# A hybrid attention and MLP layer on one core: fp32 scores ahead of the rounded ones, and transposes gathered into fewer breaks

## The chip, the core and the metric

The kernel runs on one of the cores of a Trainium2 chip. The core has a matrix engine, TensorE (PE), with a queue of weight loads that runs ahead of its matmuls (PEld), and VectorE (DVE), ScalarE (ACT), GpSimd (POOL) and SyncE (SP). TensorE writes only to PSUM, which is eight banks of 128 partitions by 512 fp32 columns. The metric is the device time of one execution in microseconds, as the median of several runs.

## The reference

256 rows of 1024 channels go through one decoder layer, all in fp32:

```python
h = rmsnorm(x, norm1_g)
proj = h @ w_in                      # q, k/v of 3 branches, gates, q/k/v of the second mixer, 2 merge gates
# mixer A: 8 heads; compressed keys (p_cmp), selected blocks, sliding window, gated and summed
y_nsa = gc[0] * (p_cmp @ vc) + gc[1] * (p_sel @ vs) + gc[2] * (p_win @ vw)
# mixer B: 8 heads of block attention; at 256 rows one block, so causal attention
y_moba = softmax(mask(qm @ km.T / 8)) @ vm
mixed = sig(g_A) * (y_nsa @ w_up_nsa) + sig(g_B) * (y_moba @ w_up_moba)
x = x + mixed @ w_out
u = relu(rmsnorm(x, norm2_g) @ w_ff1)
x = x + (u * u) @ w_ff2
return rmsnorm(x, norm_f_g)
```

## The kernel before

**Matmuls.** Large products are made in a rounded format (F32R) in three parts: each operand is split into a high part (rounded, by ScalarE, line 121) and a low part (the rest, by VectorE, line 123), and `mm3` issues high x high, high x low and low x high. Small products, the first 128 rows' scores and all transposes are plain fp32. A plain fp32 matmul appears in the trace as two instructions, a transpose as one.

**Chunks and slots.** The weights come in 60 chunks. Slot c is the run of matmuls that uses chunk c: `run_slot` walks over them (24 wide ones in the projections) and between them issues whatever was registered by `at(pos, f, ...)`, in order of `pos`: an event goes out before the first matmul whose share of the slot has reached its position. With 24 matmuls, all positions above 0.083 and up to 0.125 fall before the fourth matmul, and their order among each other is that of `pos`. Each engine works through its instructions in that program order and waits by semaphores. Such a place where PE leaves its matmuls for something else is called a break here.

**Splitting and loading.** In slot c, `std_events` and `split_events` register the high parts (`hs`) and low parts (`ls`) of the two halves of chunk c + 2, and, 0.05 behind the later low part, the load of chunk c + 5 on SP's queue: its buffer is that of chunk c + 2, so it waits for those low parts. A low part given a position above 1 is not registered there.

**Units.** Attention runs in six units d = 0 to 5, of two head pairs each. Unit d's scores are in slot 9 + 2d: `d_scores` writes tiles Sa and Sb (two banks each, one buffer each): the first 128 rows against 128 keys in fp32 (columns 0 to 127), the other rows against 256 keys rounded (columns 128 to 383). Each matmul has 64 rows of contraction, so that two use the halves of the array. Then `d_max` (VectorE: mask and maxima), `d_exp` (ScalarE), `d_norm` (VectorE, next slot); in the next odd slot `d_trans` transposes P into the same Sa and Sb, and copies them out, Sa by ScalarE (line 595), Sb by VectorE (line 596); only then can the next unit's scores be written. `d_pv` multiplies with the values a unit later. Slots 9 and 11 also transpose the second mixer's q and k (`transp_heads`, four transposes into each of two banks, line 386). The probabilities of the compressed branch, `pcs`, are transposed in slot 8 (`cmp_probs_t`, line 524) and used from slot 13 on.

**Mixed rows.** Slots 20 to 23 multiply with the two up-projections. `upn_evac` and `upm_evac` (VectorE, lines 801 to 808) merge them by the gates into `sgs[0]`, for t = 0 and 1 (the halves of the rows). `mix_t(t, i, ...)` transposes four 128-column blocks of rows t and columns half i (line 815) and makes the high part (`mxh`, ScalarE, line 819); `mix_l` makes the low part (`mxl`, VectorE, line 823). Slot 24, the first of w_out, begins with half 0 and takes half 1 in its second half.

Of the kernel before, what the change touches and what calls it, by code (L numbers as in the profile page):

```python
# [42 lines left out]
def hybrid_layer(ctx: ExitStack, tc: tile.TileContext, firstd, gxd, w, w1c, small, const, gf, out):  # L43
# [30 lines left out]
    def tp_tile():  # L74
        return next_bank("tp")
# [261 lines left out]
    def std_events(c):  # L337
        if c == 9:
            split_events(c, (0.0, 0.06), (0.09, 0.46))
        elif c == 11:  # L340
            split_events(c, (0.0, 0.1005), (0.1008, 0.1015))
        elif 9 < c < 22 and c % 2:
            split_events(c, (0.0, 0.1005), (0.09, 0.1015))
        elif 9 <= c < 20:
            split_events(c, (0.0, 0.45), (0.3, 0.8))
        else:
            split_events(c, (0.0, 0.45), (0.3, 0.46))
# [30 lines left out]
    def early_bank(t):  # L378
        return ps_e.tile([128, 512], F32, name=f"kvbacc{t}")

    def transp_heads(src, dst, i, q=True, early=None):

        tp = tp_tile() if early is None else early_bank(early)
        for j in range(2):
            for t in range(2):
                pe.transpose(tp[:, j * 256 + t * 128:j * 256 + t * 128 + 128],
                             src[:, t, (2 * i + j) * 128:(2 * i + j + 1) * 128], ident)
        v = tp.rearrange("p (a q) -> p a q", a=2)
        ps = slice(2 * i, 2 * i + 2)
        if not isinstance(dst, tuple):  # L390
            act.activation(dst[:, ps, :], v, AF.Copy)
            return
        split_evac(v, tuple(d[:, ps, :] for d in dst), q)
# [124 lines left out]
                          gates[:, 0].rearrange("q p t h -> q t p h"), op=ALU.mult)  # L518
        dve.tensor_tensor(s, s, row(3), op=ALU.mult)

    def cmp_probs_t():
        tp = tp_tile()
        for t in range(2):
            pe.transpose(tp[:, t * 128:(t + 1) * 128], pcs[:, t].rearrange("q p c -> q (p c)"),
                         ident)
        act.activation(pcT, tp[:, 0:256], AF.Copy)


    yTh = {m: ap_.tile([128, 4, 256], F32R, name=f"yTh{m}") for m in "nm"}
# [4 lines left out]

    def d_scores(d):
        S = [s_tile(x) for x in range(2)]
        rows = [slice(j * 64, (j + 1) * 64) for j in range(2)]
        late = []
        for x, (kind, p, b) in enumerate(PAIRS[d]):
            qs = qrT if kind == "n" else qmT  # L540
            kk, kp = (ksT if b == 1 else kwT, 0) if kind == "n" else (kmT, p)
            for i, (a, b_) in enumerate(((1, 1), (1, 2), (2, 1))):
                for j, r in enumerate(rows):
                    mm(S[x][:, j, 128:384], qs[a][r, p, :], kk[b_][r, kp, :], i == 0, i == 2)
            late += [(S[x][:, j, 0:128], qs[0][r, p, :], kk[0][r, kp, :])
                     for j, r in enumerate(rows)]
        for o, l, r in late:
            mm(o, l, r, True, True)
        U[d] = {"S": S, "P": ap_.tile([128, 4, 384], F32, name="P"),
                "st": ap_.tile([128, 4, 8], F32, name="ust", bufs=2)}  # L550

# [157 lines left out]
    for sec, c0, n in groups:  # L709
        if sec in ("q", "qm", "km"):  # L710
            tm[sec] = ap_.tile([128, 2, 512], F32, name="qtm", bufs=2)
        if sec == "q":
            accs = [ps_e.tile([128, 512], F32, name=f"{sec}acc{t}") for t in range(2)]
        else:
            accs = [acc_tile(), acc_tile()]
        for i in range(2):
            c = c0 + i
            if c == 4:
                for t in range(2):
                    at(0.0, evac_tm, "kvb", t, second[t], 408)  # L720
                at(0.02, cmp_gather, 0)
                at(0.02, cmp_gather, 1)
                at(0.1, split, 5, 0, 2, "l")
                at(0.2, rope, kva, 2)
                at(0.3, split, 5, 1, 2, "l")
                at(0.35, load, 8)
                at(0.72, cmp_mlp1)
                split_events(c, (0.73, 0.78), (0.8, 0.9))
            elif c == 7:
                split_events(c, (0.0, 0.1), (0.2, 0.21))  # L730
            elif c == 5:
                split_events(c, (0.115, 0.45), (0.3, 0.46))
            else:
                std_events(c)
            unit_events(c)
            v_events(c)
            if c == 5:
                at(0.05, gate_evac)
                at(0.1, transp_k, kva, ksT)
                at(0.11, cmp_gelu)  # L740
                at(0.12, rope, kvb[:, :, 0:128], 2)
                at(0.13, cmp_gelu_end)
                at(1.0, cmp_mlp2)
                at(1.0, transp_k, kvb[:, :, 0:128], kwT, 0)
            if c == 6:
                at(0.6, load_x, 0, 16 + 1024)
                at(0.68, transp_heads, tm["q"], qT, 0)
                at(0.68, transp_heads, tm["q"], qT, 1)
                at(0.7, rope, tm["q"], 8)
            if c == 7:  # L750
                at(0.25, cmp_scores)
                at(0.25, transp_heads, tm["q"], qrT, 0, True, 0)
                at(0.25, transp_heads, tm["q"], qrT, 1, True, 1)
                at(0.25, cmp_softmax)
            if c == 8:
                at(0.35, cmp_probs_t)
                at(0.3, rope, tm["qm"], 8)
            if c == 9:
                at(0.12, transp_heads, tm["qm"], qmT, 0)
                at(0.12, transp_heads, tm["qm"], qmT, 1)  # L760
            if c == 10:
                at(0.5, rope, tm["km"], 8)
            if c == 11:
                at(0.102, transp_heads, tm["km"], kmT, 0, False)
                at(0.102, transp_heads, tm["km"], kmT, 1, False)
            if i == 1:
                at(0.49, evac_tm, sec, 0, accs[0], n)
                at(1.0, evac_tm, sec, 1, accs[1], n)
            run_slot(xstat(c, n, accs, range(4 * i, 4 * i + 4)))
# [56 lines left out]
    for sec, c0, kind, evac in (("upn", C_UPN, "n", upn_evac), ("upm", C_UPM, "m", upm_evac)):  # L826
        for i in range(2):
            c = c0 + i
            if c == C_UPN:
                split_events(c, (0.3, 0.3), (0.4, 0.4))  # L830
            elif c < C_UPM:
                std_events(c)
            elif c < C_UPM + 1:
                split_events(c, (0.0, 0.0), (0.1, 0.1))
            else:
                split_events(c, (0.0, 0.0), (9, 9))
            unit_events(c)
            v_events(c)
            for f, a in prev:
                at(0.02, f, *a)  # L840
            accs = [acc_tile(), acc_tile()]
            mms = []
            for t in range(2):
                for k in range(4):
                    lh, ll = (a[kind][:, k, t * 128:(t + 1) * 128] for a in (yTh, yTl))
                    mms += mm3(accs[t], lh, ll, hi[c][:, k * 512:(k + 1) * 512],
                               lo[c][:, k * 512:(k + 1) * 512], k == 0, k == 3)
            if c == C_UPM:
                at(0.95, lambda: mix_t(0, 0, bank("yb", "yb")))
                at(0.95, mix_l, 0, 0)  # L850
            elif c > C_UPM:
                at(0.49, lambda: mix_t(1, 0, s_tile(0)[:, 0]))
                at(0.6, mix_l, 1, 0)
            at(0.52, evac, 0, i, accs[0])
            run_slot(mms)
            prev = [(evac, (1, i, accs[1]))]
# [71 lines left out]
    for i in range(4):  # L928
        c = C_WOUT + i
        if i == 0:  # L930
            at(0.03, lambda: mix_t(0, 1, bank("yb", "yb")))
            at(0.04, mix_l, 0, 1)
            at(0.25, lambda: mix_t(1, 1, s_tile(1)[:, 0]))
            at(0.26, mix_l, 1, 1)
            lo_late(0.35, c - 1)
        elif i == 1:
            lo_late(0.03, c - 1)
        split_events(c, (0.0, 0.1), ((9, 9), (0.3, 0.3), (0.3, 0.3), (9, 9))[i])
        for f, a in prev:
            at(0.02, f, *a)  # L940
        v_events(c)
        if i == 1:
            at(0.01, open_ff)
        if i == 3:
            outs = [acc_tile()[:, 0:256] for _ in range(2)]
            at(0.52, wout_evac, i, outs, (0,))
            run_slot([m for j in range(2)
                      for m in wstat(outs[j], c, j * 128, 8, 256, mxh, mxl)])
            prev = [(wout_evac, (i, outs, (1,)))]
        else:  # L950
            mms, outs, _ = two_blocks(c, mxh, mxl, 4 if i == 0 else 8, i == 0)
            run_slot(mms)
            prev = [(wout_evac, (i, outs))]
# [375 lines left out]
```

## Time and profile before

| | |
|---|---|
| Median of 3 runs | 368.4 us (367.5 to 368.4) |
| The profiled execution | 367.42 us |
| Its span, first to last instruction | 365.6 us |
| PE busy | 358.9 us (98%) |
| DVE / ACT busy | 291.7 us (80%) / 245.2 us (67%) |
| Mean granted TensorE clock | 0.995 |
| HBM read / written | 94.57 MB / 22.54 MB |

The span is what the profile sees; the device time has 1.8 us around it. Times in a timeline are from the span's start. A matmul's length in a timeline includes its way through the array, so neighbours overlap and the pace is read from their starts. The chain of work that ended last is followed back from the last instruction, at each step to what released it; its pieces follow each other without overlap, which makes their lengths good for sums.

### The profile page before, as it was taken

How to read it: one execution, taken by the hardware profiler on the slowest of the kernel's cores; microseconds unless marked ns; L12 is line 12 of the kernel's file. 1: busy time of each engine (PE TensorE's matmuls, PEld its weight loads, DVE VectorE, ACT ScalarE, POOL GpSimd, SP SyncE). 2: the span in 40 equal slices, each digit the busy share in tenths (PEclk: the TensorE clock that was granted, in tenths of full speed). 3: DMA queues.
4: the chain of work that ended last, by engine and by line, in shares of the span. 5: the costliest groups of instructions: out<-in, count | busy, mean ns of one | idle time of the engine just before them, and what ended most of it. 6: DMA issues, size and time to landing. Idle time of an engine off the chain costs nothing.

```text
span 365.6 us, 6186 instructions
## 1 busy us (share of the span) xinstructions
PE 358.9 (98%) x2370; PEld 317.6 (87%) x2370; DVE 291.7 (80%) x481; ACT 245.2 (67%) x415; POOL 49.5 (14%) x72
## 2 busy tenths in 40 slices
PE   8999999999999999999999999999999999999993
PEld 8987788888888888788999999999999888888883
DVE  5989778889786777857866788888883979999995
ACT  5976665766757557435366788888877787777814
POOL 2033003222412231313320000000000000000000
PEclk9999999999999999999999999999999999999998
DMA  8999998999999989998797765565745699999603
GB/s 259 393 396 339 321 343 256 305 261 292 266 316 249 339 169 330 231 298 192 206 350 271 233 230 162 186 229 176 261 170 174 199 326 359 367 357 341 236 0 116
DMA packets 23805, 96.01 MB, mean 263 GB/s; under 512 B 2592, under 2 KB 3616, under 8 KB 18272
## 3 DMA queue, kind: packets, MB, share of 16 engines
q1 hardware_dynamic: 14544, 73.69, 55.0%
q0 software_dynamic: 8800, 21.50, 26.9%
q10 hardware_dynamic: 432, 0.44, 0.3%
q8 instruction: 18, 0.29, 0.3%
q14 instruction: 11, 0.09, 0.1%
HBM read 94.57 MB, written 22.54 MB: 320 GB/s over the span
## 4 chain that ended last, share of the span: by engine, by line
PE 89%; DVE 4%; DMA 3%; ACT 2%; issue 1%; DVEq 0%; SPq 0%
PE acc L285 60%; PE P L285 7%; PE o L285 6%; PE qacc L285 3%; PE kvbacc L285 2%; PE yb L285 2%; DMA raw<-in_ff_dram 2%; PE Sa L285 2%; ACT whi L121 1%; PE Sb L594 1%; PE Sa L594 1%; PE Sb L285 1%; DVE x L1131 1%; PE tp L285 1%; DVE gx L1139 1%; DMA g0x<-in_first_dram 1%
## 5 line engine op out<-in xcount | busy, mean ns | idle before, releaser
L121 ACT ACTIVATE whi<-raw 128x1024 fp32r<-128x1024 f32 (+3 forms) x112 | 115.0, 1046 | 41.4 <-PE acc L285 20.9
L123 DVE TENSOR_TENSOR wlo<-raw,whi 128x1024 fp32r<-128x1024 f32 (+3 forms) x112 | 131.6, 1206 | 11.6 <-ACT whi L121 10.7
L285 PE MATMUL acc<-h2h,wlo 128*128 128x256 f32 x256 | 70.8, 276 | 0.0
L285 PE MATMUL acc<-h2l,whi 128*128 128x256 f32 x256 | 70.7, 276 | 0.0
L285 PE MATMUL acc<-h2h,whi 128*128 128x256 f32 x256 | 70.7, 276 | 0.0
L285 PE MATMUL acc<-whi,hTh 128*128 128x512 f32 (+1 forms) x128 | 49.5, 392 | 0.2 <-ACT whi L121 0.2
L285 PE MATMUL acc<-wlo,hTh 128*128 128x512 f32 (+1 forms) x128 | 48.6, 384 | 0.0
L285 PE MATMUL acc<-whi,hTl 128*128 128x512 f32 (+1 forms) x128 | 48.5, 384 | 0.0
L285 PEld LDWEIGHTS acc<-h2h,wlo 128*128 128x128 f32 x256 | 48.1, 188 | 0.0
L285 PEld LDWEIGHTS acc<-h2h,whi 128*128 128x128 f32 x256 | 48.1, 188 | 0.0
L285 PEld LDWEIGHTS acc<-h2l,whi 128*128 128x128 f32 x256 | 48.1, 188 | 0.0
L285 PEld LDWEIGHTS acc<-whi,hTh 128*128 128x128 f32 x128 | 23.9, 188 | 5.3 <-ACT whi L121 0.6
L1032 DVE TENSOR_TENSOR sql<-ur,sqh 128x512 fp32r<-128x512 f32 x16 | 11.1, 693 | 21.6 <-ACT ur L1031 21.6
L285 PEld LDWEIGHTS acc<-whi,hTl 128*128 128x128 f32 x128 | 23.8, 188 | 4.6
L285 PEld LDWEIGHTS acc<-wlo,hTh 128*128 128x128 f32 x128 | 23.9, 188 | 4.5 <-DVE wlo L123 0.3
L1151 POOL TENSOR_TENSOR fst<-fst,mhalf 128x1 f32<-128x1 f32 x1 | 0.6, 582 | 159.1 <-DVE fst L1145 159.1
L145 POOL DMA_DIRECT2D vd<-in_ff_dram x12 | 14.0, 1168 | 43.1 <-DMA vd<-in_ff_dram 43.1
L150 POOL DMA_DIRECT2D vd<-in_ff_dram x17 | 14.2, 861 | 35.2 <-DMA vd<-vd 34.6
L569 ACT ACTIVATE P<-Sa,ust 128x128 f32<-128x128 f32 (+1 forms) x24 | 9.8, 420 | 13.1 <-DVE ust L562 9.8
L1013 ACT ACTIVATE th<-vv 128x1024 fp32r<-128x1024 f32 x12 | 12.7, 1060 | 7.5 <-PE P L285 4.8
L152 POOL DMA_DIRECT2D vd<-vd x17 | 10.3, 648 | 54.8 <-DMA vd<-in_ff_dram 54.8
L1017 DVE TENSOR_TENSOR tl<-gx,th 128x1024 fp32r<-128x1024 f32 x12 | 14.7, 1226 | 3.1 <-ACT th L1013 2.4
(330 smaller groups left out, 784.4 us busy)
## 6 DMA issues: line engine op xcount, KB each, us to landing
raw<-in_ff_dram SPq DMA_DIRECT2D x18, 1024.0 KB, 4.8
vd<-in_ff_dram POOLq DMA_DIRECT2D x24, 512.0 KB, 12.1
raw<-in_ff_dram SPq DMA_DIRECT2D x12, 768.0 KB, 5.7
raw<-in_gm_dram SPq DMA_DIRECT2D x8, 1024.0 KB, 9.7
gx<-vd SPq DMA_DIRECT2D x11, 512.0 KB, 5.8
vd<-vd POOLq DMA_DIRECT2D x17, 256.0 KB, 7.3
vd<-in_ff_dram POOLq DMA_DIRECT2D x17, 256.0 KB, 7.2
raw<-in_wout_dram SPq DMA_DIRECT2D x4, 1024.0 KB, 9.5
```

The costliest lines, as they stand in the source:

```text
L121: act.activation(hi[c][:, a:b], v, AF.Copy)
L123: dve.tensor_tensor(lo[c][:, a:b], v, hi[c][:, a:b].bitcast(F32), op=ALU.subtract)
L145: pool.dma_start(v[:, 0:2], b[:, 3:4, :].to_broadcast([128, 2, 512]), accum_op=ALU.add)
L150: pool.dma_start(v[:, k], b[:, k - 2, :], accum_op=ALU.add)
L152: pool.dma_start(v[:, k], v[:, k - 1])
L285: pe.matmul(o, l, r, start=start, stop=stop, skip_group_check=True)
L569: act.activation(P[:, 2 * x + j, a:b], S[x][:, j, a:b], AF.Exp, scale=0.125, bias=st[:, 1, i:i + 1], accum_out=st[:, 2, i:i + 1])
L594: pe.transpose(S[x][:, j, c:c + 128], P[:, 2 * x + j, c:c + 128], ident)
L1013: act.activation(TT["h"][:, v], VS[c - C_FF2][:, v], AF.Copy)
L1017: dve.tensor_tensor(TT["l"][:, v], VS[c - C_FF2][:, v], TT["h"][:, v].bitcast(F32), op=ALU.subtract)
L1032: dve.tensor_tensor(l, rf, h.bitcast(F32), op=ALU.subtract)
L1131: dve.scalar_tensor_tensor(xo[:, t, s], ops[p][:, 0:n], fst[:, 4 + t:5 + t], x1[:, t, s], op0=ALU.mult, op1=ALU.add)
```

## The change

Five edits.

1. `d_scores` issues the fp32 scores of both tiles first, then the rounded ones. Before, it was the other way round.
2. The two transposes of `pcs` move from slot 8 into unit 0's scores in slot 9, ahead of them, into the free columns 384 to 511 of Sa; ScalarE copies them out behind the scores. Slot 8 has no break any more.
3. In slot 9 the eight transposes of q (`heads_t`) come ahead of the scores, their copies (`heads_evac`) behind the maxima as before.
4. The second low part of chunk 12 moves from slot 10 to slot 11, behind the transposes of P, with the load of chunk 15; the second low part of chunk 13 moves behind slot 11's maxima (0.3), and the load of chunk 16 with it (0.35). In the odd slots 13 to 21 the first low part moves from ahead of `d_trans` (0.09) to behind it (0.1012).
5. The transposes of the mixed rows: half 0 of both t in one break of slot 23 (before: t = 0 at the end of slot 22, t = 1 in slot 23); half 1 of both t in one break of slot 24 at 0.25 (before: 0.03 and 0.25). The low parts follow together.

```diff
     def std_events(c):
         if c == 9:
             split_events(c, (0.0, 0.06), (0.09, 0.46))
+        elif c == 10:
+            split_events(c, (0.0, 0.45), (0.3, 9))
         elif c == 11:
-            split_events(c, (0.0, 0.1005), (0.1008, 0.1015))
+            at(0.1006, split, c + 1, 1, 2, "l")
+            at(0.1007, load, c + 4)
+            split_events(c, (0.0, 0.1005), (0.1008, 0.3))
         elif 9 < c < 22 and c % 2:
-            split_events(c, (0.0, 0.1005), (0.09, 0.1015))
+            split_events(c, (0.0, 0.1005), (0.1012, 0.1015))
...
-    def transp_heads(src, dst, i, q=True, early=None):
-
-        tp = tp_tile() if early is None else early_bank(early)
+    HT = {}
+
+    def heads_t(src, i, early=None):
+
+        tp = HT[i] = tp_tile() if early is None else early_bank(early)
         for j in range(2):
             for t in range(2):
                 pe.transpose(tp[:, j * 256 + t * 128:j * 256 + t * 128 + 128],
                              src[:, t, (2 * i + j) * 128:(2 * i + j + 1) * 128], ident)
-        v = tp.rearrange("p (a q) -> p a q", a=2)
+
+    def transp_heads(src, dst, i, q=True, early=None):
+
+        heads_t(src, i, early)
+        heads_evac(dst, i, q)
+
+    def heads_evac(dst, i, q=True):
+
+        v = HT[i].rearrange("p (a q) -> p a q", a=2)
...
-    def cmp_probs_t():
-        tp = tp_tile()
+    def cmp_probs_t(tp):
         for t in range(2):
-            pe.transpose(tp[:, t * 128:(t + 1) * 128], pcs[:, t].rearrange("q p c -> q (p c)"),
-                         ident)
-        act.activation(pcT, tp[:, 0:256], AF.Copy)
+            pe.transpose(tp[:, t, 384:512], pcs[:, t].rearrange("q p c -> q (p c)"), ident)
...
     def d_scores(d):
         S = [s_tile(x) for x in range(2)]
+        if d == 0:
+            cmp_probs_t(S[0])
         rows = [slice(j * 64, (j + 1) * 64) for j in range(2)]
-        late = []
+        pairs = []
         for x, (kind, p, b) in enumerate(PAIRS[d]):
             qs = qrT if kind == "n" else qmT
             kk, kp = (ksT if b == 1 else kwT, 0) if kind == "n" else (kmT, p)
-            for i, (a, b_) in enumerate(((1, 1), (1, 2), (2, 1))):
+            pairs.append((x, p, qs, kk, kp))
+            for j, r in enumerate(rows):
+                mm(S[x][:, j, 0:128], qs[0][r, p, :], kk[0][r, kp, :], True, True)
+        for x, p, qs, kk, kp in pairs:
+            for i, (a, b) in enumerate(((1, 1), (1, 2), (2, 1))):
                 for j, r in enumerate(rows):
-                    mm(S[x][:, j, 128:384], qs[a][r, p, :], kk[b_][r, kp, :], i == 0, i == 2)
-            late += [(S[x][:, j, 0:128], qs[0][r, p, :], kk[0][r, kp, :])
-                     for j, r in enumerate(rows)]
-        for o, l, r in late:
-            mm(o, l, r, True, True)
+                    mm(S[x][:, j, 128:384], qs[a][r, p, :], kk[b][r, kp, :], i == 0, i == 2)
+        if d == 0:
+            act.activation(pcT.rearrange("p (t q) -> p t q", t=2), S[0][:, :, 384:512], AF.Copy)
...
             if c == 8:
-                at(0.35, cmp_probs_t)
                 at(0.3, rope, tm["qm"], 8)
             if c == 9:
-                at(0.12, transp_heads, tm["qm"], qmT, 0)
-                at(0.12, transp_heads, tm["qm"], qmT, 1)
+                for j in range(2):
+                    at(0.102, heads_t, tm["qm"], j)
+                    at(0.12, heads_evac, qmT, j)
...
-            if c == C_UPM:
-                at(0.95, lambda: mix_t(0, 0, bank("yb", "yb")))
-                at(0.95, mix_l, 0, 0)
-            elif c > C_UPM:
+            if c > C_UPM:
+                at(0.49, lambda: mix_t(0, 0, bank("yb", "yb")))
                 at(0.49, lambda: mix_t(1, 0, s_tile(0)[:, 0]))
-                at(0.6, mix_l, 1, 0)
+                for t in range(2):
+                    at(0.6, mix_l, t, 0)
...
         if i == 0:
-            at(0.03, lambda: mix_t(0, 1, bank("yb", "yb")))
-            at(0.04, mix_l, 0, 1)
+            at(0.25, lambda: mix_t(0, 1, bank("yb", "yb")))
             at(0.25, lambda: mix_t(1, 1, s_tile(1)[:, 0]))
-            at(0.26, mix_l, 1, 1)
+            for t in range(2):
+                at(0.26, mix_l, t, 1)
             lo_late(0.35, c - 1)
```

## The prediction

> **What bounds the kernel now.** I read the page's busy rows first, then the chain of work that ended last, then, around the edited lines, the timelines of TensorE, VectorE and ScalarE.
>
> ```profile
> PE 358.9 (98%) x2370; PEld 317.6 (87%) x2370; DVE 291.7 (80%) x481; ACT 245.2 (67%) x415; POOL 49.5 (14%) x72
> ...
> PEclk9999999999999999999999999999999999999998
> ...
> PE 89%; DVE 4%; DMA 3%; ACT 2%; issue 1%; DVEq 0%; SPq 0%
> ```
>
> TensorE (PE) is busy 98% of the span at full granted clock, and the chain is 89% PE. So only what PE does not have to issue or wait for can shorten the span. A busy PE can still hide lost time, so I need its steady pace. From the timeline of PE (start, length), two wide rounded matmuls 12 apart:
>
> ```profile
> 50.10 0.39 PE L285 MATMUL acc<-whi,hTl 128*128 128x512 f32 x1
> ...
> 52.82 0.39 PE L285 MATMUL acc<-whi,hTl 128*128 128x512 f32 x1
> ```
>
> (52.82 - 50.10) / 12 = 0.2267 us each. From the chain in order of time (start, length, what), the pieces around the edits:
>
> ```profile
> 53.21 0.22 PE tp L524 x2
> 53.43 4.13 PE acc L285 x18
> 57.55 0.55 PE Sa L285 x6
> 58.10 0.36 PE Sb L285 x6
> 58.46 0.22 PE Sa L285 x4
> 58.68 0.22 PE Sb L285 x4
> 58.90 1.02 PE tp L386 x8
> 59.92 10.92 PE acc L285 x48
> ...
> 72.16 0.87 PE tp L386 x8
> 73.03 0.55 PE Sa L285 x6
> 73.58 0.47 PE Sb L285 x6
> ...
> 74.50 11.12 PE acc L285 x48
> ...
> 89.37 0.48 PE Sb L285 x6
> ...
> 105.14 0.36 PE Sb L285 x6
> ...
> 162.66 0.43 PE yb L815 x4
> 163.09 2.98 PE acc L285 x13
> 166.07 0.48 PE Sa L815 x4
> 166.54 2.99 PE acc L285 x14
> 169.53 0.44 PE yb L815 x4
> 169.97 1.15 PE acc L285 x10
> 171.12 0.44 PE Sb L815 x4
> ```
>
> What a break costs beyond its own instructions: 48 steady matmuls are 48 x 0.2267 = 10.88. After a block of scores (64 of 128 rows) they take 11.12, so leaving the scores costs 0.24; after transposes 10.92, so leaving those costs 0.04. Entering the scores costs 0.55 - 0.36 = 0.19, whether rounded matmuls stand ahead (57.55) or fp32 transposes (73.03). Eight transposes take 0.87 (0.109 each), but 1.02 behind scores: 0.15 for that exit.
>
> **The change part by part.** *Slots 8 and 9* (one break less; scores after the transposes). Before: slot 8's break is 0.22 for two transposes and 4.13 - 18 x 0.2267 = 0.05 behind them; slot 9's block is 0.55 + 0.36 + 0.22 + 0.22 + 1.02 + 0.04 = 2.41. Together 2.68. After: the same ten transposes 0.22 + 0.87 with rounded matmuls ahead, the scores with their entry 1.35, and the exit, now into rounded matmuls, 0.24: 2.68. The saved break is paid back by the dearer exit: 0.0, between -0.05 and +0.05.
>
> *Order inside the scores*, six units. The same instructions, so the only question is the type change. Now it stands at the exit (fp32 to rounded, 0.24); afterwards it is inside the block and the exit is rounded to rounded. No row shows such an exit. The nearest rows say the height of the array in use sets the price and not the type: the entry at 57.55, rounded to rounded, costs the same 0.19 as the one at 73.03, and the exit at 58.90, fp32 to fp32, 0.15. From rounded to fp32 inside the block (58.46) costs nothing now (0.22 for two pairs of 0.109); the other direction is bounded by 0.04, the one after transposes. I take 0; the bounds are 6 x 0.04 = 0.24 lost and, if a type change did make the exit dear, 6 x (0.24 - 0.04) = 1.2 gained.
> The Trainium skill, TensorEngine Tiling (Array Packing), section Key Properties, says that changing the tiling mode drains TensorE. By that rule the number of drains is unchanged, two in a unit, and the sum keeps its 0 here; by the other reading it would have the 1.2.
>
> *VectorE's order around the maxima*. In slots 11 and 13 the second score tile took 0.47 and 0.48, in slot 15 only 0.36. VectorE (DVE) and ScalarE around them:
>
> ```profile
> 71.30 1.22 DVE L123 TENSOR_TENSOR wlo<-raw,whi 128x1024 fp32r<-128x1024 f32 x1
> 72.43 0.95 DVE L596 COPY PT<-Sb 128x768 f32<-128x768 f32 x1
> ...
> 84.81 3.49 DVE L123 TENSOR_TENSOR wlo<-raw,whi 128x1024 fp32r<-128x1024 f32 x3
> 88.22 0.95 DVE L596 COPY PT<-Sb 128x768 f32<-128x768 f32 x1
> ```
>
> The copy that frees Sb stands behind a low part and ends at 73.38 and 89.17; Sb's matmuls wait. Afterwards the low part is behind the copy. Slot 11: the transposes into Sb end at 72.16, so the copy can run from 72.2 to 73.15. Sb's first matmuls, now the fp32 ones, are due at 73.03 + 0.19 + 0.22 = 73.44, sooner than the rounded ones were (73.58). Before, a copy that ended at 73.38 held those back by 0.47 - 0.36 = 0.11, to 73.69: the copy has to end some 0.31 ahead. 73.15 + 0.31 = 73.46, so the margin is near zero and I book 0.11 less 0.03. Slot 13: the third low part of that 3.49 goes behind, so the copy ends about 1.2 sooner than 89.17, far ahead of need: 0.12. Sum 0.20; bounds 0 and 0.25.
>
> Where the moved low parts go, and what they might delay:
>
> ```profile
> 82.36 0.17 DVE L574 TENSOR_SCALAR ust<-ust 128x8 f32<-128x8 f32 x1 [1.79 <-ACT P L569]
> ...
> 65.98 0.17 DVE L574 TENSOR_SCALAR ust<-ust 128x8 f32<-128x8 f32 x1 [1.18 <-ACT P L569]
> ```
>
> Chunk 13's second half (1.21) falls behind slot 11's maxima, into VectorE's idle 1.79 while the exponentials run. Chunk 12's second half takes its place ahead of them, done near 73.15 + 1.22 = 74.4 and used in slot 12, 21 matmuls after 74.5, at 79.3. In slot 9 Sa now ends at 57.55 - 0.27 + 1.09 + 0.19 + 0.44 + 0.36 = 59.36 instead of 58.68. The new copy of the compressed probabilities out of Sa, on ScalarE, is a third of the one of 0.81 at 86.31 below: 0.4 as an estimate, and behind it wait only the copies of the q heads, which units read from slot 17 on. So the maxima start at most 0.7 + 0.4 = 1.1 later; the idle 1.18 ahead of 65.98 takes that. All 0; without that cover slot 11's transposes of P would come later by the rest.
>
> The SP queue: chunk 15's load is now issued behind chunk 12's late low part, at about 74.4 instead of the 72.54 below; chunk 16's behind chunk 13's, near 81.6 (the maxima's end at 82.36 - 1.79 = 80.57, 0.2 sooner, and 1.21).
>
> ```profile
> 72.54 0.33 SPq L98 DMA_DIRECT2D raw<-in_gm_dram  x1
> DMA to landing us min/median/max: 9.9/9.9/9.9
> ...
> DMA to landing us min/median/max: 10.8/10.8/10.8
> ...
> 85.02 1.06 ACT L121 ACTIVATE whi<-raw 128x1024 fp32r<-128x1024 f32 x1 [0.22 <-ACT whi L121]
> 86.31 0.81 ACT L595 ACTIVATE PT<-Sa 128x768 f32<-128x768 f32 x1 [0.23 <-PE Sa L594]
> ```
>
> The two loads took 9.9 and 10.8 us. Chunk 15 lands at 84.3 to 85.2 and is first read at 85.02: just in time, with 16 no longer beside it. Chunk 16 lands by 92.4, read at slot 14's start near 95 (89.37 + 0.48 + 0.44, and 21 matmuls). Cost 0.
>
> *Mixed rows*, four breaks to two. The four take 0.43 + 0.48 + 0.44 + 0.44 = 1.79 against 16 x 0.109 = 1.74, and the matmuls behind them 2.98 against 13 x 0.2267 = 2.95, 2.99 against 2.95 (12 wide, 2 half as wide at half the pace, an estimate), 1.15 against 1.13, and say 0.02 behind the last: 0.16 in all, 0.05 of it a wait in the second. Two breaks like the first, 0.03 each, leave 0.06: 0.10 gained; bounds 0 and 0.16. The low part of t = 0 joins that of t = 1 on VectorE:
>
> ```profile
> 167.44 0.68 DVE L823 SCALAR_TENSOR_TENSOR mxl<-Sa,mxh 128x512 fp32r<-128x512 f32 x1
> ```
>
> With 0.69 more behind 168.12 it ends by 168.8; w_out's matmuls begin 0.23 ahead of the break at 169.53 and use it as the second. Hidden by some 0.5. In w_out's first slot the joint break stands where the later of its two stood, and PE reaches t = 1 there 0.03 sooner than at 171.12, so ready times hold.
>
> Sum: 0.0 + 0 + 0.20 + 0.10 = 0.30 us, on the profiled execution: 367.42 (span 365.6 and 1.8 around it) to 367.1. Its time is 1.0 below the median shown, 368.4 (367.5 to 368.4). Against that median: 368.4 - 0.3 = **368.1**.
>
> Does a gain on PE reach the end? The tail of the chain:
>
> ```profile
> 328.89 1.06 ACT th L1013
> ...
> 333.80 8.40 DMA raw<-in_ff_dram
> ```
>
> From 328.9 the chain runs over a load and then ScalarE and VectorE, but that piece starts from PE, so it shifts with it; a landing of 8.4 us that varies by some tenths can swallow the 0.3.
>
> **The rivals.** *The type change is what makes the exit dear*: 1.2 more, 368.4 - 1.5 = 366.9, faster. For it: 0.24 behind fp32 scores against 0.04 behind transposes. Against: the entry at 57.55 between rounded and rounded, and the 0.15 between fp32 and fp32. *Nothing arrives*: six type changes inside the blocks cost their 0.24, or the tail's load or VectorE keeps its time: 368.4 or a tenth off it. *Chunk 15 is late*: its rounding on ScalarE at 85.02 stands ahead of the copy that frees Sa. Landing at t, the copy ends at t + 1.06 + 0.81; the scores of slot 13 enter near 88.8 (0.55 before Sb's 89.37), so it decides from t = 86.9, a landing of 12.5 us, and PE then stalls for all beyond. At one and a half times 10.8 (16.2, t = 90.6) that is 3.7 lost, 368.4 - 0.3 + 3.7 = 371.8, slower. Against: the two rows, and one load less beside it.
>
> **How the numbers follow.** About 0.3% (1.1 us) is what a measurement of this kernel can tell from no change. Forecast 0.62, nothing arrives 0.16, both within that bound: 0.78 same. Type change 0.12, and 0.03 for gains of the other parts at their upper bounds with it in part: 0.15 faster. Late chunk 0.04, and 0.03 for a wait I have not seen: 0.07 slower. Range: down to the type-change case, 366.8, up to no gain and the spread of runs, 369.0. The forecast's own range is 367.2 (367.5 less 0.3) to 368.5.
>
> **What would show it.** Right: Sb's first matmuls in slots 11 and 13 without a wait; 48 matmuls after a unit still 11.12; slot 8 without a break; two breaks of eight transposes near 165 and 170; chunk 15 rounded near 85. Wrong: 48 matmuls in 10.9 after the units (type change), PE idle ahead of slot 13's scores (late chunk), or any idle of PE at slot 9's or 11's transposes.

## The result, and the profile after

The changed kernel takes 371.46 us (371.34 to 371.91), the kernel before 368.4 us (367.5 to 368.64), five runs each. The ratio is 1.0091 with a 95% interval of 1.0076 to 1.0106. It is slower by about 0.9%, where I had forecast 0.3 us faster with a range up to 369.0.

The page of the changed kernel, the rows that answer to those of before. The last three are groups of 256 matmuls or weight loads (PEld) of the first MLP product; their columns are busy us, mean ns of one, and idle time before.

```profile
span 370.0 us, 6183 instructions
...
PE 363.3 (98%) x2370; PEld 323.1 (87%) x2370; DVE 291.6 (79%) x481; ACT 245.2 (66%) x415; POOL 49.4 (13%) x72
...
PEclk9999999999999999999999999999999999999999
...
PE 97%; DMA 1%; DVE 1%; ACT 0%; issue 0%
...
L285 PE MATMUL acc<-h2h,wlo 128*128 128x256 f32 x256 | 72.0, 281 | 0.0
...
L285 PEld LDWEIGHTS acc<-h2l,whi 128*128 128x128 f32 x256 | 49.1, 192 | 0.0
...
L285 PEld LDWEIGHTS acc<-h2h,wlo 128*128 128x128 f32 x256 | 48.1, 188 | 0.0
```

The first two of these groups on the page before:

```profile
L285 PE MATMUL acc<-h2h,wlo 128*128 128x256 f32 x256 | 70.8, 276 | 0.0
...
L285 PEld LDWEIGHTS acc<-h2l,whi 128*128 128x128 f32 x256 | 48.1, 188 | 0.0
```

The span grew by 4.4 us and PE's busy time by as much, for the same 2370 instructions on PE at the same granted clock. No other engine has more work. PE does not wait longer; it works more slowly. The matmuls of the first MLP product last 281 ns instead of 276, and one weight load in three lasts 192 ns instead of 188. The prediction had not looked at that stage at all.

The chain in order of time (start, length, what) of the changed kernel:

```profile
4.22 2.10 PE acc L285 x6
...
58.81 0.42 PE Sa L285 x4
59.23 0.22 PE Sb L285 x4
59.45 0.35 PE Sa L285 x6
59.81 0.36 PE Sb L285 x6
60.16 11.10 PE acc L285 x48
71.27 0.66 PE Sa L609 x6
...
73.45 0.42 PE Sa L285 x4
73.87 0.24 PE Sb L285 x4
74.12 0.36 PE Sa L285 x6
74.48 0.36 PE Sb L285 x6
74.83 11.11 PE acc L285 x48
...
170.90 0.44 PE yb L830 x4
171.34 0.44 PE Sb L830 x4
171.77 110.83 PE acc L285 x941
```

And two pieces of the chain of the kernel before:

```profile
4.16 1.44 PE acc L285 x6
...
171.56 106.66 PE acc L285 x941
```

The last lines hold the whole loss. From the last break of slot 24 to the break in the first MLP product's last slot (43, seven matmuls from its end) the same 941 narrow matmuls (256 columns) take 110.83 us instead of 106.66. That is 117.8 ns from start to start instead of 113.3, and 4.17 us. Up to slot 24 the changed kernel is ahead: from the first matmul of q (start 22.42 before, 22.85 after) to the first of w_out (169.13 and 169.32) it takes 146.47 us instead of 146.71, 0.24 less. The 0.43 that it lags at q's start comes from the kernel's first six matmuls (2.10 us instead of 1.44, partly made up for later); that start lies between 22.20 and 23.07 in the traces of the runs below, whatever the kernel, so executions differ by it. Without that lag the two traces are 3.9 us apart. The two medians are 3.1 us apart, but the kernel before, measured again beside the later runs, took 367.76 us (31 executions) and 367.81 (21), which makes some 3.7.

The pace is regular from the first narrow matmul on. The timeline of PE in the changed kernel, at the start of slot 24 and behind its break:

```profile
169.32 0.28 PE L285 MATMUL acc<-mxh,whi 128*128 128x256 f32 x1
169.44 0.28 PE L285 MATMUL acc<-mxl,whi 128*128 128x256 f32 x1
...
171.96 0.28 PE L285 MATMUL acc<-mxh,whi 128*128 128x256 f32 x1
172.08 0.28 PE L285 MATMUL acc<-mxl,whi 128*128 128x256 f32 x1
```

The same place before the change:

```profile
169.13 0.28 PE L285 MATMUL acc<-mxh,whi 128*128 128x256 f32 x1
169.25 0.29 PE L285 MATMUL acc<-mxl,whi 128*128 128x256 f32 x1
169.37 0.60 PE L815 MATMUL yb<-ident,sga 128*128 128x128 f32 x4
...
170.28 0.28 PE L285 MATMUL acc<-mxh,whi 128*128 128x256 f32 x1
170.39 0.28 PE L285 MATMUL acc<-mxl,whi 128*128 128x256 f32 x1
```

Both kernels start slot 24 slowly, some 0.12 us from start to start. Before, a break of four transposes follows after two matmuls, and a few matmuls behind it the pace is 0.113. After the change the first break comes after twelve, with eight transposes, and the pace stays 0.118 behind it.

### The profile page after: what moved, and what is told of

It reads as the page before. It is cut to its first block, busy times and chain, and to the rows that moved or that the text cites. A ratio compares the mean times of both kernels' runs of the same rounds, so it can differ in the third digit from the quotient of the medians.

```text
span 370.0 us, 6183 instructions
## 1 busy us (share of the span) xinstructions
PE 363.3 (98%) x2370; PEld 323.1 (87%) x2370; DVE 291.6 (79%) x481; ACT 245.2 (66%) x415; POOL 49.4 (13%) x72
## 4 chain that ended last, share of the span: by engine, by line
PE 97%; DMA 1%; DVE 1%; ACT 0%; issue 0%
PE acc L285 60%; PE o L285 12%; PE P L285 9%; PE qacc L285 3%; PE yb L285 3%; PE kvbacc L285 2%; PE Sa L285 2%; PE Sa L609 1%; PE Sb L609 1%; PE Sb L285 1%; PE tp L285 1%; DMA g0x<-in_first_dram 1%; PE tp L392 1%; PE o L938 0%; PE kvbacc L392 0%; PE tp L444 0%
## 5 line engine op out<-in xcount | busy, mean ns | idle before, releaser
L285 PE MATMUL acc<-h2h,wlo 128*128 128x256 f32 x256 | 72.0, 281 | 0.0
L285 PE MATMUL acc<-h2l,whi 128*128 128x256 f32 x256 | 71.9, 281 | 0.0
L285 PE MATMUL acc<-h2h,whi 128*128 128x256 f32 x256 | 71.9, 281 | 0.0
L285 PEld LDWEIGHTS acc<-h2l,whi 128*128 128x128 f32 x256 | 49.1, 192 | 0.0
```

The lines of the kernel that those rows point to most:

```text
L285: pe.matmul(o, l, r, start=start, stop=stop, skip_group_check=True)
```

## The experiments

I call 113.3 ns the fast pace and 117.8 ns the slow one. They were read from the starts of neighbouring narrow matmuls; no third lasting pace appeared in any run. The diffs here are shortened: statements on lines of their own are joined by semicolons, and `...` stands for what is left out.

**Which edit brings the slow pace?** Four kernels.

`e1_mix_four`: the change without its fifth edit.

```diff
-            if c > C_UPM:
-                at(0.49, lambda: mix_t(0, 0, ...)); at(0.49, lambda: mix_t(1, 0, ...))
-                for t in range(2): at(0.6, mix_l, t, 0)
+            if c == C_UPM:
+                at(0.95, lambda: mix_t(0, 0, ...)); at(0.95, mix_l, 0, 0)
+            elif c > C_UPM:
+                at(0.49, lambda: mix_t(1, 0, ...)); at(0.6, mix_l, 1, 0)
...
-            at(0.25, lambda: mix_t(0, 1, ...)); at(0.25, lambda: mix_t(1, 1, ...))
-            for t in range(2): at(0.26, mix_l, t, 1)
+            at(0.03, lambda: mix_t(0, 1, ...)); at(0.04, mix_l, 0, 1)
+            at(0.25, lambda: mix_t(1, 1, ...)); at(0.26, mix_l, 1, 1)
```

> The changed kernel with its fifth edit undone: the mixed rows' transposes stand in four breaks again, the other four edits stay. The trace after the change shows the 256-column matmuls of w_out and of the first MLP product at 117.8 ns from start to start, before the change 113.3 ns; 941 of them make the 4.2 us. Theory A, the place of the breaks in slots 22 to 24 sets that pace: 113.3 ns here, and the time is that of before less the local gains of the other edits (0.1 to 0.3 us): 368.1 us, ratio 0.999. Rival B, something that the other edits shift (the units, the loads, VectorE's order) sets it: 117.8 ns here too, 371.5 us, ratio 1.009.

Measured: 367.77 us, ratio 1.0001 (0.9992 to 1.0011), fast pace. Rival B falls: the units, the loads and VectorE's order don't bring the slow pace alone.

`e3_slot24_as_before`: only the second half of that diff.

> The changed kernel, but the two breaks of slot 24 as before (after 2 and after 12 of its matmuls); slot 23 keeps the joint break. Theory A1, the break after two matmuls of slot 24 is what puts the narrow matmuls at the fast pace: 113.3 ns after it, 368.0 us, ratio 0.999. Theory A2, the joint break in slot 23 leaves TensorE in the slow pace, whatever follows: 117.8 ns, 371.5 us, ratio 1.009.

Measured: 367.69 us, ratio 1.0001 (0.9987 to 1.0014), fast pace. A2 falls as it was put: slot 23's joint break doesn't bind what follows.

`e5_slot24_join_only`: the kernel before, with slot 24's breaks joined and nothing else.

```diff
-            at(0.03, lambda: mix_t(0, 1, ...)); at(0.04, mix_l, 0, 1)
-            at(0.25, lambda: mix_t(1, 1, ...)); at(0.26, mix_l, 1, 1)
+            at(0.25, lambda: mix_t(0, 1, ...)); at(0.25, lambda: mix_t(1, 1, ...))
+            for t in range(2): at(0.26, mix_l, t, 1)
```

> The kernel before with one thing changed: slot 24's two breaks joined into one after 12 matmuls; slots 8 to 23 are those of before. Theory A1 (the early break of slot 24 set the fast pace): 117.8 ns through the first MLP product, 368.4 + 4.2 - 0.1 = 372.5 us by the profile's sum, 371.5 us by the difference measured, ratio 1.008 to 1.011. Rival A2 or B (slot 23's joint break, or the other edits): 113.3 ns, 368.4 us, ratio 1.000.

Measured: 367.78 us, ratio 0.9999 (0.9989 to 1.0010), fast pace. So A1 falls too: without the early break of slot 24 the pace can still turn fast. Its chain, with the same breaks in slot 24 as the changed kernel:

```profile
170.89 0.44 PE yb L815 x4
171.32 0.44 PE Sb L815 x4
171.76 106.67 PE acc L285 x941
```

`e2_mix_only`: the kernel before with the whole fifth edit, so `e5` and the joint break of slot 23.

> The kernel before with the whole fifth edit (joint breaks in slots 23 and 24) and none of the others. Joining slot 24's breaks alone left the narrow matmuls at 113.3 ns. If the two joint breaks together are enough for the slow pace: 117.8 ns, ratio 1.009, 371.3 us. If it takes the exact timing that all five edits give together (theory P: the pace is a state that a break shuffles, with the outcome set by fine timing): 113.3 ns, ratio 1.000, 367.7 us. P does not say which of the two comes out here, only that it is one of these two paces; a third pace speaks against it.

Measured: 371.59 us, ratio 1.0096 (1.0081 to 1.0111), slow pace: the fifth edit alone is enough. The other four edits are not needed for the loss. But `e5` and `e2` have the same slot 24 and differ only in where slots 22 and 23 break, a slot or more earlier, and in when the low part that belongs to the moved break is made. Both enter slot 24 at 0.118 from start to start, so the pace ahead of a break does not decide the pace behind it.

**Does the place of slot 24's break decide?** The changed kernel with the break after 13, 14 and 15 matmuls instead of 12.

```diff
-            at(0.25, lambda: mix_t(0, 1, ...)); at(0.25, lambda: mix_t(1, 1, ...))
-            for t in range(2): at(0.26, mix_l, t, 1)
+            at(0.28, lambda: mix_t(0, 1, ...)); at(0.28, lambda: mix_t(1, 1, ...))   # 0.27 and 0.3 in the others
+            for t in range(2): at(0.29, mix_l, t, 1)
```

> The changed kernel with slot 24's joint break two matmuls later (after 14 instead of 12). Nothing else differs. If the slow pace is a matter of where in a cycle of three weight loads the break falls (every third load takes 192 ns instead of 188 in the slow stretch), the break can end it here: 113.3 ns behind it and 368.0 us. If a joint break of eight transposes never ends it, or the first matmuls of slot 24 decide: 117.8 ns and 371.5 us.

> The changed kernel with slot 24's joint break after 13 matmuls (12 in the change, 14 in an earlier run, which was fast). If the place in a cycle of three decides, 13 is a place of its own and 15 is that of 12; P leaves both outcomes open: 113.3 ns and 367.4 us, or 117.8 ns and 371.3 us.

> The changed kernel with slot 24's joint break after 15 matmuls. If the place of the break in the cycle of three weight loads decides, 15 is the same place as 12: 117.8 ns behind it and 371.3 us, ratio 1.009. If the exact time of the break decides and not its place in the cycle, the usual outcome (five of the six kernels so far): 113.3 ns and 367.4 us.

Measured: after 14 matmuls 367.3 us, ratio 0.9995 (0.9984 to 1.0005), fast; after 13, 371.72 us, ratio 1.0100 (1.0085 to 1.0115), slow; after 15, 371.84 us, ratio 1.0103 (1.0086 to 1.0119), slow. Two matmuls' difference in one position takes the whole loss away. Taken alone, these four places (12 and 15 alike) fit the theory of a cycle of three; `e5`, fast with the same place 12, does not, nor do the 42 breaks of one transpose below. The last part of the chain with 14:

```profile
171.63 106.44 PE acc L285 x939
```

All kernels entered slot 24 at the slow pace. Behind the first break there:

| kernel | slot 23 | first break of slot 24 | pace behind it |
|---|---|---|---|
| before, `e1` | four | four, after 2 | fast |
| `e3` | eight | four, after 2 | fast |
| `e5` | four | eight, after 12 | fast |
| changed, `e2` | eight | eight, after 12 | slow |
| `e6` | eight | eight, after 13 | slow |
| `e4`, `e14` | eight | eight, after 14 | fast |
| `e7` | eight | eight, after 15 | slow |

**Is the pace a state, or a property of the program?** The changed kernel with four extra breaks in the first MLP product.

```diff
+    PROBES = {2: 1, 5: 2, 8: 4, 11: 8}
+    def probe(n):
+        tp = bank("yb", "yb")
+        for _ in range(n):
+            pe.transpose(tp[:, 0:128], ident, ident)
...
+        if i in PROBES:
+            at(0.5, probe, PROBES[i])
```

> The changed kernel with extra breaks in the first MLP product, each after 24 of a slot's 48 matmuls: 1 transpose of the identity in slot 30, 2 in slot 33, 4 in slot 36, 8 in slot 39 (15 transposes, 1.6 us of added work whose result nobody reads). Theory P (the pace is a state that lasts while narrow matmuls follow each other without a break): 117.8 ns up to one of these breaks, 113.3 ns from it to the end; if the first does it, some 650 matmuls gain 4.4 ns each, 2.9 us, and the kernel takes 371.4 + 1.6 - 2.9 = 370.1 us, if the last, 371.4 + 1.6 - 1.0 = 372.0 us. Rival Q (the pace is a fixed property of this program, such as where its operands or instructions lie): 117.8 ns throughout and 373.0 us.

Measured: 370.9 us, ratio 1.0077 (1.0060 to 1.0094). The chain of that kernel:

```profile
171.36 35.34 PE acc L285 x300
206.69 0.11 PE yb L1064
206.80 16.34 PE acc L285 x144
223.14 0.22 PE yb L1064 x2
223.36 16.96 PE acc L285 x144
240.32 0.44 PE yb L1064 x4
240.76 16.34 PE acc L285 x144
257.10 0.87 PE yb L1064 x8
257.97 23.71 PE acc L285 x209
```

Length divided by count: 117.8 ns, then behind one transpose 113.5 (a few slower matmuls right behind the break are counted in), behind two 117.8, behind four 113.5, behind eight 113.4. The same kind of matmul on the same kind of operands runs at either pace, and each break may change it, in both directions. Rival Q is out. Theory P holds in that the pace lasts between breaks; that it would stay fast to the end, once changed, was wrong, as the break of two changed it back.

**What about a break decides?** The changed kernel with 42 breaks of one, two or four transposes.

```diff
+        if 0 < i < 15:
+            for pos in (0.25, 0.52, 0.79):
+                at(pos, probe, 1)        # 2 and 4 in the others
```

> The changed kernel with 42 extra breaks of one identity transpose each in the first MLP product: slots 29 to 42, after 12, 25 and 38 matmuls (4.6 us of added work nobody reads; the time counts for nothing here). Read is the pace before and behind each break. In the run with four breaks one transpose led from 117.8 to 113.3 ns, two from 113.3 to 117.8, four from 117.8 to 113.3, eight stayed at 113.3. Theory N, the number of transposes decides: fast behind all 42. Theory M, the place in the cycle of three decides: 12, 25 and 38 (remainders 0, 1, 2) differ from each other and each is always alike. Theory F, fine timing decides: both paces at every place.

> As the run before with two transposes in each of the 42 breaks. Theory N: slow (117.8 ns) behind all 42. Theory M: alike at each place. Theory F: both paces at every place.

> As the run before with four transposes in each of the 42 breaks. Theory N: fast (113.3 ns) behind all 42, which is also what four of four breaks of this size in w_out's first slot did. Theory M: alike at each place. Theory F: both paces at every place.

These added transposes make 376.38, 380.93 and 387.62 us (one run each; before 367.97). Counted from the starts in the traces, the steady pace ahead of each break and behind it:

| transposes in the break | slow to fast | slow to slow | fast to fast | fast to slow |
|---|---|---|---|---|
| 1 | 9 | 20 | 4 | 9 |
| 2 | 1 | 40 | 0 | 1 |
| 4 | 1 | 1 | 40 | 0 |

None of the three theories comes through whole. N holds as a tendency: fast behind 41 of 42 breaks of four, slow behind 41 of 42 of two. These are not 42 independent trials: from the third break of four on, the starts behind each break follow at the same distances (202, 116, 118, 122, 119, 113 ns), so one pattern repeats itself. With one transpose both paces occur, and eight in slot 24 gave both. So did the break of 16 transposes in slot 43, which every kernel has: the seven matmuls behind it run at the slow pace in the kernel before, the changed one and seven others, at the fast pace in the other seven. M fails: with one transpose, place 25 (the break after 25 matmuls) was slow behind all 14, but places 12 and 38 gave both. F is right that both occur at one place, but it isn't chance: from slot 31 on, the one-transpose breaks at place 12 go slow-to-fast, fast-to-fast, slow-to-slow and round again, one step each slot. What quantity that is a phase of stays open.

**Can the kernel before be slowed the same way?** No edit of the change, one break in slot 30.

```diff
+        if i == 2:
+            at(0.5, probe, 2)        # 4 in the other
```

> The kernel before, none of the five edits, with one extra break of two identity transposes in slot 30, after 24 of its 48 matmuls (0.22 us of added work nobody reads). If the pace is a state that a break sets (theory P), and breaks of two lead from fast to slow as in both cases seen so far: 117.8 ns from there to the end of the first MLP product, some 650 matmuls at 4.4 ns, 2.9 us: 367.9 + 0.2 + 2.9 = 371.0 us, ratio 1.008. If the slow pace belongs to the edits: 113.3 ns and 368.1 us, ratio 1.001.

> As the run before, with four transposes in the break (0.44 us of added work). Theory P, with breaks of four as seen in the 42 of one run: the pace stays at 113.3 ns and the kernel takes 367.9 + 0.4 = 368.3 us, ratio 1.001: more added work than with two, less time. If added work in slot 30 costs by itself: more than with two.

Measured: with two transposes 371.0 us, ratio 1.0084 (1.0070 to 1.0098); with four 368.58 us, ratio 1.0017 (1.0007 to 1.0027). Both as expected. The chain with two:

```profile
171.52 34.02 PE acc L285 x300
205.53 0.22 PE yb L1048 x2
205.75 75.50 PE acc L285 x641
```

and with four:

```profile
171.57 34.02 PE acc L285 x300
205.59 0.44 PE yb L1048 x4
206.02 72.68 PE acc L285 x641
```

Two transposes of 0.22 us cost 2.8 us behind them that four don't. So the slow pace needs no edit of the change: a break in slot 30 alone brings it.

**What are the edits worth by themselves?** The kernel of `e4` again, measured eleven times.

> The changed kernel with slot 24's joint break after 14 instead of 12 matmuls, once more with more rounds: 113.3 ns in the narrow stage. Here the five edits' own gains must show, by the chain 0.2 to 0.3 us: 367.7 us, ratio 0.9993. If they are lost on the way: ratio 1.000.

Measured: 367.73 us, ratio 0.9997 (0.9986 to 1.0009). From q's first matmul to the end of the span it takes 342.97 us, the kernel before 343.19: 0.22 less. That is a gain that the trace shows and the time can't tell from none. No version tried here is faster than the kernel before by more than the measurement is uncertain.

## Why the prediction was wrong

The direction and the range failed in one step, the sum of the mixed rows. "Two breaks like the first, 0.03 each, leave 0.06" priced a break by what stood right behind it, until the pace was steady again, and took for granted that the steady pace is one number: 0.2267 us for wide matmuls and "half as wide at half the pace, an estimate" for narrow ones. For narrow ones there are two steady paces. The term that the prediction put at nothing, without a row for it, is 941 x (117.8 - 113.3) = 4.2 us, lost or not by the state that the last break leaves. Why a given break leaves one state or the other stays open. The trace before showed signs, at both ends of the narrow stretch: slot 24's first two matmuls, 0.12 apart, and the seven behind slot 43's break, 0.118 apart, are slower than the 941 between. I read over both. Two starts of the latter, in the kernel before:

```profile
280.05 0.28 PE L285 MATMUL acc<-h2l,whi 128*128 128x256 f32 x1
280.17 0.28 PE L285 MATMUL acc<-h2h,wlo 128*128 128x256 f32 x1
```

None of the rivals named it; the 0.03 for "a wait I have not seen" was the nearest, and it wasn't a wait.

The other steps, each by its own line:

- *Slots 8 and 9, 0.0*: right. From 47.05 to the transposes of P at 70.85 before, 23.80 us; after, from 47.48 to 71.27, 23.79.
- *Order inside the scores, 0*: right. Leaving the scores, now from rounded to rounded, is followed by 48 matmuls in 11.10 to 11.11 us in five units (11.15 in slot 13), instead of 11.11 to 11.12. So the type had no part in the exit's cost, and the rival of a 1.2 us gain falls. The entry is 0.42 - 0.22 = 0.20 instead of 0.19, and fp32 to rounded inside the block costs nothing (0.35 and 0.36). The Trainium skill's rule that a change of the tiling mode drains TensorE (TensorEngine Tiling (Array Packing), Key Properties) fits the trace: both changes of a unit still cost about what they did, 0.20 going in (0.19 before) and, in five units, 0.22 to 0.23 coming out (0.24).
- *VectorE's order, 0.20*: nearly right. Slot 11's scores take 0.42 + 0.24 + 0.36 + 0.36 = 1.38 instead of 1.46, with 0.02 of a wait left in Sb, as the narrow margin said. From P's transposes in slot 11 to those in slot 13 the kernel saves 0.10; in slot 13's stretch 0.08 (101.64 - 85.94 = 15.70 against 15.78), where I had 0.12. The 0.04 that is missing stands behind the scores: the 48 matmuls there take 11.15 us, because eleven steps from start to start, instead of five behind slot 11's scores, are off the steady 0.2267.
- *Covers on VectorE*: right. The low part moved behind the maxima starts at 80.67 and fits ahead of the next unit's work.

```profile
80.67 1.22 DVE L123 TENSOR_TENSOR wlo<-raw,whi 128x1024 fp32r<-128x1024 f32 x1
82.55 0.17 DVE L589 TENSOR_SCALAR ust<-ust 128x8 f32<-128x8 f32 x1 [0.66 <-ACT P L584]
```

- *Chunk 15's load*: right. It is issued at 74.73 and lands by 84.5; its rounding starts at 85.34, behind PE's last matmul of slot 12 and not behind the load, so the late-chunk rival didn't happen:

```profile
DMA to landing us min/median/max: 9.4/9.4/9.4
...
85.34 1.06 ACT L121 ACTIVATE whi<-raw 128x1024 fp32r<-128x1024 f32 x1 [0.35 <-PE acc L285]
```

- *Mixed rows, 0.10 by breaks alone*: about half. From 148.38 to w_out's first matmul 20.75 us before, from 148.62 to it 20.70 after. Two runs separate the edits: from q's first matmul to w_out's first, `e1` (the first four) takes 146.53 us and `e2` (the fifth) 146.66, so 0.18 and 0.05 of the 0.24. The join in slot 24 gains nothing: slot 24 takes 6.39 us in `e5`, where it alone is changed, and 6.37 before.
- *A gain on PE reaches the end*: right where the pace is fast; `e14` is 0.26 ahead at slot 24 and keeps 0.22. The rest goes in slot 24 (6.40 us instead of 6.37), whose first 14 matmuls run at the slow pace. The chain of the changed kernel stays on PE to the end (97%) and no longer runs over the load at 333.80, but from slot 43's break to the end both traces take 85.88 us. The doubt about that load was sound: in `e13` it took 9.16 us instead of 8.40, and the same stretch 86.58.

## What to carry to other kernels

Where PE is the bound, compare its pace stage by stage, as matmuls over time in the chain, also in stages that the edit doesn't touch, before any break or wait is weighed. In a long run of matmuls with a new weight load for each, whose loads follow each other without idle time, a break at its head, or even one a slot ahead, can decide by 4% how fast all of them run. This was seen for one shape only, 256 columns. A disturbance of other size or place at the head of that run (here the joint break two matmuls later, or two breaks of four) is a cheap trial. And an edit that shows a loss may be innocent: its time has to be compared with that of a neighbour that differs only in such timing.

## What the runs showed of the hardware that I had not expected

Narrow matmuls (256 columns, rounded, a new load of 128 columns each) keep one of two paces, 113.3 or 117.8 ns, for up to 941 matmuls, with the mean granted clock at 0.995 to 0.998 in all traces. At the slow pace one weight load in three takes 192 ns, the others 188. Which of the three it is belongs to no operand: it stands with the product of the low part and the high weights (`h2l,whi`) in the changed kernel, of high and high (`h2h,whi`) in `e6`, of high and low (`h2h,wlo`) in `e12`. All kernels begin slot 24, behind the wide matmuls, at the slow pace, and only a break of fp32 transposes was seen to change the pace after that. Wide matmuls (512 columns) come back to 226.7 ns within some ten matmuls of a break: their loads (188 ns) have 39 ns of idle time between them, those of narrow ones have none (0.0 on the page). That this missing slack is why a narrow stream can't recover is my reading and was not tried. The Trainium skill (TensorE: Matmul & The Clock Gate, Back-to-back issue gap) says that the spacing in a stream of load and matmul pairs is set by both; no run here separates the two. Its formula for a matmul alone gives 256/2.4 + 2.5 = 109 ns (an estimate), which is neither of the paces measured.

As far as the times tell, a program keeps its pace in all its executions: the five of the changed kernel lie within 0.6 us of each other, and no execution of the kernel before took more than 368.8 us.
